# Reciprocal square roots by one third-order step and one Newton step instead of three Newton steps

## The chip, the cores and the metric

The kernel runs on one core of a Trainium2 chip. The metric is the time on the device in microseconds (us); the median of several runs counts. The profile names the engines: PE is TensorE (its weight loads are PEld), DVE is VectorE, ACT is ScalarE, POOL is GpSimd, SP is SyncE, which issues most of the transfers.

## What is computed

The reference is one layer of an encoder over 2048 positions of width 1024. `x` goes through an RMS norm and one input projection. That yields queries, keys and values of two attention mixers (A: a window of 128; B: three groups of heads with dilations 1, 4 and 16), gate paths and merge gates. Every head's query and key has an RMS norm of its own:

```python
def rms_norm(x, gain):
    xf = x.astype(jnp.float32)
    y = xf * lax.rsqrt(jnp.mean(xf * xf, axis=-1, keepdims=True) + EPS)
    return (y * gain.astype(jnp.float32)).astype(x.dtype)

h = rms_norm(x, norm_gain[layer])
proj = h @ w_in[layer]
qa, ka, va, qb, kb, vb, ga, gb, mg = jnp.split(proj, split_idx, axis=-1)
qa = head_rms_norm(qa.reshape(bsz, S, A_Q_HEADS, HEAD_DIM), q_norm_a[layer]) * scale
ka = head_rms_norm(ka.reshape(bsz, S, A_KV_HEADS, HEAD_DIM), k_norm_a[layer])
...
merged = gates[:, :, 0] * br_a + gates[:, :, 1] * br_b
x = x + merged @ w_out[layer]
```

The reciprocal square root of these norms is what the change touches.

## The kernel before

All matmuls take float16 operands, and a float32 operand is split into a high and a low part (`wh`, `wl` for weights, `XH`, `XL` for the normed and transposed `x`), so that one product becomes three.

**The start.** `x` comes in 16 tiles of 128 rows. ScalarE squares a tile and sums its rows (L450), VectorE turns the sums into means and makes a first guess of the root from the bits of the number (L454, `rs_guess` L263), `x_newton` refines it (`rs_newton`), VectorE scales the tile (`x_scale`, L464), TensorE transposes it (L470), ScalarE and VectorE write the high and the low part (L473, L477). The roots are made in five groups: tiles 0 and 1, tiles 2 and 3 (both on VectorE, `pool` False), then four tiles each (on GpSimd, `pool` True).

**The main part** goes through 14 units (two of mixer A, twelve of mixer B), each with 8 pairs of blocks of 128 rows: 112 pairs. For a pair TensorE projects two blocks into two PSUM banks (L655, 48 matmuls). Then follows one round of small work, planned in `Pair.plan`:

- ScalarE copies queries and keys out (L673) and the high part of the values (L688); VectorE writes the low part of the values (`v_lo`, L694), which is the last reader of the PSUM bank;
- ScalarE squares (L701), VectorE sums per head (L706, L707) and makes the guess (L263);
- GpSimd refines the root (`newton`, L272 to L275), 12 instructions on 8 or 10 numbers a partition; the last writes `qr`;
- VectorE multiplies by it (`scale`, L718), GpSimd by the gain (L725), ScalarE and VectorE split the product (L731, L735), GpSimd swaps two halves (L740), and a transposing DMA writes the result into the ring `kq`, out of which ScalarE copies an edge (L758, L764).

Meanwhile the items of the attention run: scores on TensorE (L833), bias and maximum on VectorE (L848), the exponential on ScalarE (L856), a split (L861, L865), a transposing DMA, the products with the values on TensorE (L882), and merges of the heads (GpSimd L1001, L1041; VectorE L1023 to L1048). GpSimd also multiplies the next unit's weights by the gain (`gains`, L182) and those of gate columns (L326). Between the pairs of some units stand whole gate projections (`FILLS`, L310).

**The order.** Everything between `order.enter_context(tc.manual_schedule())` and the end is issued in an order written out by hand: `at(t, f)` puts a step on a heap under a planned time `t` counted in pairs, and `until(t)` issues all steps that are due. Each engine works through its instructions strictly in that order; the planned times decide nothing else. The delays of a pair's steps after its second block are

```python
NORM = (0.028, 0.136, 0.32, 0.626, 0.744, 0.904, 0.962, 1.033, 1.118)
...
steps = (self.square, self.stats, self.newton, self.scale, self.gain, self.hi, self.lo, self.swap, self.turn)
for d, f in zip(NORM, steps):
    at(e[1] + d, f)
```

so that on VectorE the split L735 of one pair stands ahead of L694 and L706 of the next, and L718 ahead of L735.

**The end** (from some 1378 us) makes the rest of the gates, the branch products and the output projection, by TensorE products of half blocks (L1440, L1645), without any of the roots above.

Of the kernel before, what the change touches and what calls it, by code (L numbers as in the profile page):

```python
# [25 lines left out]
OP = mybir.AluOpType  # L26
# [87 lines left out]
def block_kernel(tc, x, w_units, w_gate, w_mrg, w_brn, w_out, w_bra, gain, qkg, sink, bias_a, bias_b, b_merge, out):  # L114
    nc = tc.nc
    V = nc.vector
    A = nc.scalar
    G = nc.gpsimd
# [147 lines left out]
    def rs_newton(a, yv, r, n, pool):  # L266

        t = sm.tile([128, 10], F32, name="rs_t")
        tv = t[:, :n]
        for i in range(3):  # L270
            if pool:
                G.tensor_tensor(tv, yv, yv, OP.mult)  # L272
                G.tensor_tensor(tv, tv, a, OP.mult)  # L273
                G.tensor_scalar(tv, tv, -0.5, 1.5, OP.mult, OP.add)  # L274
                G.tensor_tensor(r if i == 2 else yv, tv, yv, OP.mult)  # L275
                continue
            V.tensor_tensor(tv, yv, yv, OP.mult)
            V.scalar_tensor_tensor(tv, tv, -0.5, a, OP.mult, OP.mult)
            V.scalar_tensor_tensor(r if i == 2 else yv, tv, 1.5, yv, OP.add, OP.mult)


    zd = [dr.tile([2, S, 132], F32, name=f"zd{p}") for p in range(4)]
# [174 lines left out]
    def x_newton(g):  # L457
        ss, y = xss[g]
        xss[g] = sm.tile([128, 4], F32, name="xr")
        rs_newton(ss, y, xss[g][:, :len(g)], len(g), len(g) > 2)  # L460
# [178 lines left out]
    class Pair:  # L639
# [70 lines left out]
        def newton(self):  # L710
            n = 2 * self.nh
            self.rr = sm.tile([128, 10], F32, name="qr")
            rs_newton(*self.ss, self.rr[:, :n], n, True)
# [1064 lines left out]
```

## Time and profile before

| | |
|---|---|
| median of 3 runs | 1948.53 us (1947.81 to 1949.16) |
| profiled execution | 1949.46 us |
| its span, first to last instruction | 1947.7 us |
| mean granted TensorE clock | 0.996 |
| L272, GpSimd | 345 instructions, median 202 ns, 104.9 us busy in all |
| L273, GpSimd | 345, medians 204 and 201 ns |
| L274, GpSimd | 345, median 198 ns |
| L275, GpSimd | 345, medians 200 to 203 ns |
| L277 to L279, VectorE | 18, medians 160 to 161 ns |
| GpSimd's idle time ahead of L272, for the guess L263 | 153.1 us in 86 waits |
| GpSimd's idle time ahead of L725, for L718 | 62.1 us in 69 waits |

The page gives for each engine its busy time and the share of the span; the chain that ended last follows the work back from the last instruction, at each step to what released it. A row of the timeline has the start, the duration, engine, line, operation, and the tile written `<-` those read; in brackets stands how long the engine was idle before it and what released it. A row of waits has the sum, the number and the longest of the waits. A row of windows has the length of the window, then for PE, PEld, DVE, ACT and POOL the busy time and, in brackets, the instructions, then the granted TensorE clock, the share of the DMA engines and GB/s.

### The profile page before, as it was taken

The page shows a single profiled execution, that of the slowest core. Times are in us where ns is not written, and L with a number is a line of the kernel's source. Part 1 is how long each engine was busy: PE and PEld are TensorE (multiplying, and loading weights), DVE is VectorE, ACT ScalarE, POOL GpSimd, SP SyncE. Part 2 cuts the span into 40 slices and gives each one's busy share as a digit, 9 for nine tenths or more (in the row PEclk, how much of TensorE's full clock was granted, in tenths as well). Part 3 has the DMA queues.
Part 4 walks back from the last instruction along what each step waited for, and adds up shares of the span by engine and source line. Part 5 has one row for each costly group of instructions (what it writes and reads, how often), then busy time and mean ns, then how long its engine had stood idle before and what let it go on. Part 6 is the DMA issues. An engine that isn't in the chain of part 4 may idle for free.

```text
span 1947.7 us, 40273 instructions
## 1 busy us (share of the span) xinstructions
PE 1923.5 (99%) x13702; PEld 1211.9 (62%) x13702; DVE 1373.0 (70%) x3604; ACT 1073.4 (55%) x2451; POOL 953.4 (49%) x2440
## 2 busy tenths in 40 slices
PE   7999999999999999999999999999999999999999
PEld 5556676677766688566787567876544444444444
DVE  6668787888767776677876878768776756876422
ACT  7457666776565566665666656666534545422100
POOL 4254456445546756647666676656511310232533
PEclk8999999999999999999999999999999999999999
DMA  6239977797858596677767776765822246778763
GB/s 252 82 75 174 192 154 158 137 188 147 189 96 189 117 189 124 127 147 163 159 130 147 138 173 123 144 120 115 187 82 96 99 157 202 217 236 269 248 243 140
DMA packets 589743, 307.96 MB, mean 158 GB/s; under 512 B 458081, under 2 KB 527329, under 8 KB 588257
## 3 DMA queue, kind: packets, MB, share of 16 engines
q1 hardware_dynamic: 571104, 296.73, 64.7%
q10 hardware_dynamic: 18432, 8.66, 1.9%
q8 instruction: 107, 1.75, 0.4%
q14 instruction: 100, 0.81, 0.1%
HBM read 129.91 MB, written 65.27 MB: 100 GB/s over the span
## 4 chain that ended last, share of the span: by engine, by line
PE 49%; DVE 4%; POOL 3%; issue 2%; ACT 1%; DMA 1%; SPq 0%; DVEq 0%; POOLq 0%
PE pj L655 16%; PE fps L310 13%; PE fps L1645 7%; PE pj L310 6%; PE fps L1440 5%; PE s L833 1%; PE pv L882 1%; POOL rs_t L272 1%; POOL rs_t L273 1%; DVE rw L718 1%; DVE qss L706 1%; POOL rs_t L274 1%; DMA kq<-spl 0%; POOL rs_y L275 0%; DVE pr L848 0%
## 5 line engine op out<-in xcount | busy, mean ns | idle before, releaser
L655 PE MATMUL pj<-wh,XH 128*128 128x384 f16 x1792 | 584.7, 326 | 6.2 <-DVE vt L694 6.2
L655 PE MATMUL pj<-wh,XL 128*128 128x384 f16 x1792 | 586.6, 327 | 0.0
L655 PE MATMUL pj<-wl,XH 128*128 128x384 f16 x1792 | 585.2, 327 | 0.0
L655 PEld LDWEIGHTS <-XH 128*128 128x128 f16 x3584 | 412.9, 117 | 155.1 <-issue 8.1
L848 DVE CUSTOM_DVE_ANT_0 pr<-s,b,ubuf 128x256 f32<-128x256 f32 (+3 forms) x512 | 218.4, 463 | 51.3 <-PE s L833 49.9
L655 PEld LDWEIGHTS <-XL 128*128 128x128 f16 x1792 | 207.8, 116 | 68.8 <-issue 0.2
L272 POOL TENSOR_TENSOR rs_t<-rs_y 128x8 f32<-128x8 f32 (+2 forms) x345 | 104.9, 304 | 211.9 <-DVE rs_y L263 153.1
L865 DVE SCALAR_TENSOR_TENSOR p<-pr,p 128x512 f16<-128x512 f32 (+2 forms) x256 | 185.9, 726 | 25.1 <-ACT p L861 24.2
L718 DVE TENSOR_TENSOR rw<-rw,qr 128x512 f32<-128x512 f32 (+1 forms) x112 | 110.8, 989 | 88.0 <-POOL vt L681 56.9
L725 POOL TENSOR_TENSOR rw<-rw,g 128x128 f32<-128x128 f32 (+1 forms) x224 | 128.9, 596 | 76.5 <-DVE rw L718 62.1
L310 PEld LDWEIGHTS <-wh 128*128 128x128 f16 x960 | 93.8, 98 | 111.4 <-issue 1.5
L861 ACT ACTIVATE p<-pr 128x512 f16<-128x512 f32 (+2 forms) x256 | 159.2, 622 | 6.3
L740 POOL COPY spl<-spl 128x256 f16<-128x256 f16 (+1 forms) x224 | 93.5, 447 | 130.4 <-DVE spl L735 128.9
L310 PE MATMUL fps<-Y,wh 128*128 128x512 f16 x512 | 152.3, 379 | 0.0
L833 PE MATMUL s<-kq 128*128 128x256 f16 (+3 forms) x1168 | 147.8, 254 | 2.0 <-ACT kq L758 2.0
L882 PEld LDWEIGHTS <-pt 128*128 128x128 f16 x3024 | 126.0, 98 | 35.0 <-issue 0.3
L310 PE MATMUL pj<-XH,gl 128*128 128x512 f16 x384 | 146.0, 380 | 0.0
L310 PE MATMUL pj<-XH,gh 128*128 128x512 f16 x384 | 146.0, 380 | 0.0
L310 PE MATMUL pj<-XL,gh 128*128 128x512 f16 x384 | 145.9, 380 | 0.0
L673 ACT ACTIVATE rw<-pj 128x256 f32<-128x256 f32 (+1 forms) x224 | 86.3, 385 | 107.8 <-PE pj L655 94.9
L1645 PE MATMUL fps<-wt,M 128*128 128x512 f16 (+1 forms) x684 | 145.2, 375 | 0.0
L731 ACT ACTIVATE spl<-rw 128x512 f16<-128x512 f32 (+1 forms) x112 | 72.1, 644 | 122.3 <-POOL vt L681 80.5
(245 smaller groups left out, 3679.9 us busy)
## 6 DMA issues: line engine op xcount, KB each, us to landing
wraw<-in_w_units_dram SPq DMA_DIRECT2D x56, 384.0 KB, 4.9
mtd<-mm SPq DMA_DIRECT2D x56, 256.0 KB, 3.8
M<-mtd SPq DMA_DIRECT2D x8, 1792.0 KB, 9.2
mgd<-fg SPq DMA_DIRECT2D x39, 256.0 KB, 2.1
zd<-z ACTq DMA_DIRECT2D x128, 66.0 KB, 2.5
zz<-zd SPq DMA_DIRECT2D x64, 132.0 KB, 2.8
xt<-in_x_dram SPq DMA_DIRECT2D x16, 512.0 KB, 8.6
gtd<-yo SPq DMA_DIRECT2D x32, 256.0 KB, 2.8
```

The source lines that it names most:

```text
L272: G.tensor_tensor(tv, yv, yv, OP.mult)
L310: out.append(lambda w=w, xx=xx, ch=ch, i=i: T.matmul(ps[:], lhsT=w[:, ch, c0:c0 + 128], rhs=xx[:, ch, ts], start=(i == 0), stop=(i == n - 1)))
L655: out.append(lambda lhs=lhs, rhs=rhs, ch=ch, k=k: T.matmul(ps[:, :384], lhsT=lhs[:, ch, :], rhs=rhs[:, ch, :], start=(k == 0), stop=(k == ...
L718: V.tensor_tensor(q, q, self.rr[:, :n].unsqueeze(2).to_broadcast([128, n, HD]), OP.mult)
L725: G.tensor_tensor(q[:, i, :un.nq, :], q[:, i, :un.nq, :], g, OP.mult)
L833: T.matmul(self.sv[j][:, o:o + k1 - k0], lhsT=q[:, h, qo:qo + 128], rhs=kt[:, un.nq + kh + v * un.nk, k0:k1], start=(v == 0), stop=(v == 1))
L848: V.tensor_tensor_reduce(out=self.pv[:, j, self.p0:self.p0 + W], in0=self.sv[j], in1=un.bias[:, self.h0 + j, self.b0:self.b0 + W], scale=I ...
L861: A.activation(self.sp[:, :128 * n], self.pr, AF.Copy, scale=PSC)
L865: V.scalar_tensor_tensor(self.sp[:, 128 * n:], self.pr, PSC, self.sp[:, :128 * n], OP.mult, OP.subtract)
L882: T.matmul(self.po[:, j, :w], lhsT=p[:, n * j + s, :], rhs=un.v[key][:, vh, c0:c0 + w], start=(k == 0 and s == 0), stop=(k == 2 and s == n ...
L1440: mm.append(lambda ch=ch, k=k, w=w, i=i: T.matmul(ps[:], lhsT=weight(bl, ch)[w], rhs=xblock(x, ch)[k], start=(i == 0), stop=(i == 11)))
L1645: mm.append(lambda ch=ch, k=k, w=w, i=i: T.matmul(ps[:, :cols.stop - cols.start], lhsT=m[:, a, ch, k, :], rhs=wt[w][:, b, ch, cols], start ...
```

## The change

`rs_newton` gets the mean `a` and a guess `yv` of its reciprocal square root. Before, it makes three times the step y = y (1.5 - 0.5 a y y). Now, with t = a y y, it makes one step y = y (1.875 - 1.25 t + 0.375 t t) and then one step as before. On GpSimd the twelve instructions become ten, with `r` as a place for what lies between; on VectorE, where an instruction can do two operations on three operands, nine become seven. Nothing else changes, and no other line is moved in the written order.

```diff
         t = sm.tile([128, 10], F32, name="rs_t")
         tv = t[:, :n]
-        for i in range(3):
-            if pool:
-                G.tensor_tensor(tv, yv, yv, OP.mult)
-                G.tensor_tensor(tv, tv, a, OP.mult)
-                G.tensor_scalar(tv, tv, -0.5, 1.5, OP.mult, OP.add)
-                G.tensor_tensor(r if i == 2 else yv, tv, yv, OP.mult)
-                continue
-            V.tensor_tensor(tv, yv, yv, OP.mult)
-            V.scalar_tensor_tensor(tv, tv, -0.5, a, OP.mult, OP.mult)
-            V.scalar_tensor_tensor(r if i == 2 else yv, tv, 1.5, yv, OP.add, OP.mult)
+        if pool:
+            G.tensor_tensor(tv, yv, yv, OP.mult)
+            G.tensor_tensor(tv, tv, a, OP.mult)
+            G.tensor_scalar(r, tv, 0.375, -1.25, OP.mult, OP.add)
+            G.tensor_tensor(r, r, tv, OP.mult)
+            G.tensor_scalar(r, r, 1.875, None, OP.add)
+            G.tensor_tensor(yv, r, yv, OP.mult)
+            G.tensor_tensor(tv, yv, yv, OP.mult)
+            G.tensor_tensor(tv, tv, a, OP.mult)
+            G.tensor_scalar(tv, tv, -0.5, 1.5, OP.mult, OP.add)
+            G.tensor_tensor(r, tv, yv, OP.mult)
+            return
+        V.tensor_tensor(tv, yv, yv, OP.mult)
+        V.scalar_tensor_tensor(tv, tv, 0.375 ** 0.5, a, OP.mult, OP.mult)
+        V.scalar_tensor_tensor(tv, tv, -1.25 * 0.375 ** -0.5, tv, OP.add, OP.mult)
+        V.scalar_tensor_tensor(yv, tv, 1.875, yv, OP.add, OP.mult)
+        V.tensor_tensor(tv, yv, yv, OP.mult)
+        V.scalar_tensor_tensor(tv, tv, -0.5, a, OP.mult, OP.mult)
+        V.scalar_tensor_tensor(r, tv, 1.5, yv, OP.add, OP.mult)
```

## The prediction

> **What bounds the kernel now.** I read the page first: its busy times, then its chain that ended last.
>
> ```profile
> span 1947.7 us, 40273 instructions
> ...
> PE 1923.5 (99%) x13702; PEld 1211.9 (62%) x13702; DVE 1373.0 (70%) x3604; ACT 1073.4 (55%) x2451; POOL 953.4 (49%) x2440
> ...
> PE 49%; DVE 4%; POOL 3%; issue 2%; ACT 1%; DMA 1%; SPq 0%; DVEq 0%; POOLq 0%
> PE pj L655 16%; PE fps L310 13%; PE fps L1645 7%; PE pj L310 6%; PE fps L1440 5%; PE s L833 1%; PE pv L882 1%; POOL rs_t L272 1%; POOL rs_t L273 1%; DVE rw L718 1%; DVE qss L706 1%; POOL rs_t L274 1%; DMA kq<-spl 0%; POOL rs_y L275 0%; DVE pr L848 0%
> ```
>
> TensorE is busy for 99% of the span: at most some 24 us of the whole can be won by anything that leaves its matmuls alone. But the lines of the reciprocal square root on GpSimd (L272 to L275) stand in the chain with about 1% each, so in some stretches TensorE does wait for them. To find the stretches I asked for TensorE's waits in three windows: 60 to 1000 us, 1000 to 1200, 1200 to 1450.
>
> ```profile
> PE pj L655 <- DVE vt L694: 0.7, 2, 0.4
> ```
> ```profile
> PE pj L655 <- DVE vt L694: 3.6, 3, 2.0
> PE s L833 <- ACT kq L758: 1.7, 2, 1.2
> ```
> ```profile
> PE pj L655 <- DVE vt L694: 1.9, 1, 1.9
> PE pt L944 <- DVE ya L1048: 0.7, 1, 0.7
> PE s L833 <- ACT kq L758: 0.3, 1, 0.3
> ```
>
> L694 frees the projection's PSUM bank. VectorE runs in the written order, and there L694 stands behind L718, which multiplies by the result `qr`. L758 copies transposed keys that come out of the same round. So these 8.9 us (0.7 + 3.6 + 1.7 + 1.9 + 0.7 + 0.3) of TensorE's idleness are the prize. What L718 waits for:
>
> ```profile
>   POOL vt L681: 56.9, 37
> ```
>
> The memset L681 is queued right behind the last step of the root; L718 starts at that step's end (below, 1075.80 + 0.20 against 1076.04), so the row is a wait for `qr` under another name.
>
> The chain that ended last, in the windows 1050 to 1130 and 1280 to 1380, leaves TensorE and returns to it as follows; between the two ends stand whole roots on GpSimd.
>
> ```profile
> 1059.72 0.20 PE pv L882 x6
> ...
> 1062.74 0.32 POOL rs_t L272
> ...
> 1114.05 0.20 POOL rs_t L272
> ...
> 1125.33 1.30 PE pj L655 x7
> ```
> ```profile
> 1283.79 0.20 PE pv L882 x6
> ...
> 1286.33 0.32 POOL rs_t L272
> ...
> 1361.16 0.20 POOL rs_t L272
> ...
> 1377.40 0.62 PE s L833 x8
> ```
>
> From 1062.74 to 1114.05 it passes six roots, from 1286.33 to 1361.16 nine (one of them for three steps only). A round (row sums, guess, root, scale, gain, split, and the next row sums behind it on VectorE) takes (1114.05 - 1062.74) / 5 = 10.3 us there and (1361.16 - 1286.33) / 8 = 9.4 in the second stretch; TensorE went through ten pairs before at 8.9 us each (1066.39 - 977.45, rows below), so the rounds are the slower part.
>
> **The change, part by part.**
>
> **GpSimd.** Twelve instructions become ten: seven tensor by tensor and three tensor by scalar where there were nine and three. Their price, from the timeline of one root:
>
> ```profile
> 1072.58 0.31 POOL L272 TENSOR_TENSOR rs_t<-rs_y 128x8 f32<-128x8 f32 x1 [0.40 <-DVE rs_y L263]
> ...
> 1073.26 0.20 POOL L274 TENSOR_SCALAR rs_t<-rs_t 128x8 f32<-128x8 f32 x1
> ...
> 1073.82 0.20 POOL L272 TENSOR_TENSOR rs_t<-rs_y 128x8 f32<-128x8 f32 x1
> ...
> 1075.80 0.20 POOL L275 TENSOR_TENSOR qr<-rs_t,rs_y 128x8 f32<-128x8 f32 x1
> ```
>
> From the fifth to the twelfth start are 1.98 us for seven steps, 0.283 us a step, whichever of the two kinds. Two steps fewer are 0.57 us a root: 3.43 becomes 2.86 us. Where VectorE stretches a step of the root, the stretch belongs to the VectorE instruction beside it and not to the number of steps, so I keep 0.57 everywhere. The one-operation tensor by scalar (add 1.875, no second operation) stands in no row; I take it at the 0.20 of L274, and for its ends 0.1 either way (0.1 x 15 roots = 1.5 us at the most). That `r` is now written from the third step on could add a wait only for the L718 that reads the same buffer, four pairs back; at 8.9 us a pair that is long done: nothing.
>
> **VectorE** (the first two x groups, two tiles each): nine become seven.
>
> ```profile
> 7.52 0.16 DVE L277 TENSOR_TENSOR rs_t<-rs_y 128x2 f32<-128x2 f32 x1
> ...
> 9.09 0.16 DVE L279 SCALAR_TENSOR_TENSOR xr<-rs_t,rs_y 128x2 f32<-128x2 f32 x1
> ```
> ```profile
> 11.99 1.06 ACT L450 ACTIVATE jk<-xt 128x1024 f16<-128x1024 f32 x1 [1.69 <-DMA xt<-in_x_dram]
> ```
>
> Eight steps in 1.57 us are 0.196 each, so 0.39 us a group. What hides it is ScalarE: it splits the first tile only behind the square that stands at 11.99 and waits for a load, and that load does not come sooner. I cost it at nothing; without that cover it would be 0.4 to 0.8 us.
>
> **The third x group, on GpSimd,** is not hidden:
>
> ```profile
> 25.64 1.49 DVE L464 TENSOR_SCALAR xt<-xt,xr 128x1024 f32<-128x1024 f32 x1 [1.72 <-POOL xr L275]
> ```
> ```profile
> 27.27 0.30 PE L470 MATMUL s<-idf,xt 128*128 128x128 f32 x1 [1.93 <-DVE xt L464]
> ```
>
> VectorE waits 1.72 us for the root and TensorE 1.93 us for VectorE; both shrink by 0.57. I count 0.6 us.
>
> **The stretch 1059 to 1125.** Its six roots alone give 6 x 0.57 = 3.4 us. It gives more, because the rounds were already falling behind before TensorE first stood still:
>
> ```profile
> 977.45 0.33 PE L655 MATMUL pj<-wh,XH 128*128 128x384 f16 x1
> ```
> ```profile
> 978.75 0.69 DVE L706 TENSOR_REDUCE qss<-spl 128x8 f32<-128x512 f32 x1 [0.23 <-ACT spl L701]
> ```
> ```profile
> 1066.39 0.33 PE L655 MATMUL pj<-wh,XH 128*128 128x384 f16 x1
> ```
> ```profile
> 1071.35 0.67 DVE L706 TENSOR_REDUCE qss<-spl 128x8 f32<-128x512 f32 x1
> ```
>
> The row sums L706 came 1.3 us after the next pair's first matmul at 977, and 5.0 us after it ten pairs later. Ten roots less by 0.57 are 5.7 us, more than the 3.7 lost; but a round that has caught up can't run ahead of TensorE, so part of that is wasted. I estimate that 2.3 of the 3.7 us are gone by 1071. Five more roots up to the release at 1125.33 add 2.85: the chain arrives 5.2 us sooner. The waits of the window sum to 5.3 (3.6 + 1.7), and a short spell at half clock adds to what TensorE could give back, so the chain, not TensorE, still sets that end: 5.2 us. Ends: 3.4 and 7.0. Late next there: L694 behind L735, as now, by a fraction.
>
> **The stretch 1284 to 1377.** Eight whole roots are 4.6 us, the waits there 1.9 + 0.7 + 0.3 = 2.9. TensorE is the limit: 2.9. If L1048 and the key transposes are late for another reason, 1.9.
>
> **The two early waits** (0.7 us in 60 to 1000): one root each covers 0.4; 0.7. Other end 0.
>
> **All other roots** lie beside a busy TensorE: nothing. Their cover is the 99%; without it they would be 0.57 each.
>
> **The clock.** Half clock shows in two windows of 3.4 us:
>
> ```profile
> 1110.10:1113.60 3.50, 1.51 (x10) 0.78 (x8) 3.43 (x10) 2.61 (x8) 1.89 (x5) 1.00 0.65 137
> 1113.60:1117.00 3.40, 3.40 (x23) 2.28 (x22) 3.03 (x15) 3.14 (x9) 2.29 (x9) 0.50 1.09 101
> ```
> ```profile
> 24.70:28.10 3.40, 1.47 (x12) 1.01 (x11) 2.46 (x3) 1.17 (x3) 1.63 (x5) 1.00 1.03 391
> 28.10:31.50 3.40, 3.40 (x14) 2.00 (x12) 2.24 (x10) 3.25 (x7) 0.00 (x0) 0.51 1.03 399
> ```
>
> In each, a window with TensorE busy for about 1.5 us is followed by one at half clock, which costs 1.7 us of matmuls. The first spell I have inside the 7.0 above. The second may go, since TensorE would be busy 0.57 us longer in the window before it; I leave it out of the sum and put 1.7 into the range. The Trainium skill, "TensorE: Matmul & The Clock Gate", section "What's actually happening", says that the clock falls to half after at least one idle window of about 3.4 us, and that this window runs free of the kernel's start. Its length agrees with the rows; its condition does not (1.5 us of 3.4 were busy). By its condition alone neither spell would be there and 1.7 us less would be at stake; the sum stays as it is.
>
> Sum: 0.6 + 5.2 + 2.9 + 0.7 = 9.4 us. The profiled execution took 1949.46 us, 0.93 above the runs' median of 1948.53. Less 9.4 that is 1940.1, or 1939.1 from the median; I say 1939.5. A measurement tells about 0.2%, 3.9 us, from no change.
>
> **Rivals.**
>
> *TensorE-bound, nothing comes of it.* For it: 99% busy, and TensorE's listed waits are short. Against it: both chains above run through GpSimd. It would leave the start alone, 1948.53 - 0.6 = 1947.9.
>
> *A smaller gain.* The rounds before 1059 win nothing that lasts, the early waits stay, and in the late stretch only L694's wait goes: 3.4 + 1.9 = 5.3, so 1943.2. For it: the key transposes (DMA) stand in the late chain.
>
> *A larger gain.* All waits and both spells go: 0.6 + 1.7 + 7.0 + 2.9 + 0.7 = 12.9, so 1935.6.
>
> *Slower: VectorE's scale is stretched more often.* L718 beside another GpSimd multiplication and alone:
>
> ```profile
> 1066.17 1.47 POOL L182 TENSOR_TENSOR wraw<-wraw,gn 128x768 f32<-128x768 f32 x1
> ```
> ```profile
> 1066.21 1.98 DVE L718 TENSOR_TENSOR rw<-rw,qr 128x512 f32<-128x512 f32 x1 [1.91 <-POOL vt L681]
> 1076.04 0.69 DVE L718 TENSOR_TENSOR rw<-rw,qr 128x512 f32<-128x512 f32 x1 [2.33 <-POOL vt L681]
> ```
>
> A root that ends sooner lets the next GpSimd instruction start sooner. If that puts a weight multiplication beside L718, or beside another VectorE instruction of the round, where there is none now, the round loses 1.98 - 0.69 = 1.29 and wins 0.57. In all fifteen roots of the two chains that is 15 x 0.72 = 10.8, less the 1.3 of start and early waits: 1958.0. It decides from eleven such rounds on (11 x 1.29 = 14.2 against 9.4 + 3.9). Against it: where L718 waits for `qr`, both engines' next work moves by the same 0.57, and their order in time stays. The Trainium skill, "SBUF — State Buffer", section "Who interferes with whom", has the rule behind this: a VectorE instruction with two inputs in SBUF and a GpSimd instruction that reads SBUF exclude each other, the later one waiting for the earlier one's end. The trace agrees: 1.47 + 0.69 = 2.16 in turn, 1.98 measured.
>
> **How the numbers follow.** Chances: the forecast 0.46, the smaller gain 0.20, the larger 0.15, nothing 0.14, slower 0.05. Of the first three all but 0.01 lie over 3.9 us: faster 0.80, within 0.15, slower 0.05. The range runs from the larger gain, 1935.5, past the smaller to 1945.5, and leaves out most of "nothing" and the slower case. The forecast's own ends: 1936 to 1943.
>
> **What would show it.** Right: a root of ten steps in 2.9 us; `xr` ready by 25.1 us and the transpose by 26.8; under 1 us of waits for L694 in all; no more chain through L272 to L275 between 1284 and 1377, and shorter passages before 1125. Wrong: steps longer than 0.283 us, L694 waited for as before, or new L718 durations near 2 us. What would break it: waits that move to L1048 or the key transposes by as much.

## The result, and the profile after

The changed kernel takes 1937.75 us (median of 6 runs, 1937.26 to 1941.01) where the kernel before took 1948.17 beside it (6 runs, 1945.95 to 1949.51): the ratio over all runs is 0.9951, 95% interval 0.9938 to 0.9963 (the two medians alone give 0.9947). That is 10.4 us less; the forecast was 1939.5. The profiled execution is the longest of the six, 1941.01 us with a span of 1939.2.

The page after, span, busy times and the chain that ended last:

```profile
span 1939.2 us, 40047 instructions
...
PE 1921.7 (99%) x13702; PEld 1211.1 (62%) x13702; DVE 1377.2 (71%) x3600; ACT 1075.9 (55%) x2451; POOL 900.6 (46%) x2210
...
PE 88%; DVE 4%; DMA 3%; issue 2%; POOL 1%; ACT 1%; SPq 1%; ACTq 0%; DVEq 0%; POOLq 0%
PE pj L664 41%; PE pj L319 14%; PE fps L319 10%; PE fps L1654 7%; PE s L842 5%; PE fps L1449 5%; PE pv L891 4%; PE pt L953 1%; PE s L479 1%; DMA fg<-ytd 1%; DMA xt<-in_x_dram 0%; DMA kq<-spl 0%; DVE rw L727 0%; DVE qss L715 0%; DMA b<-in_bias_a_dram 0%
```

TensorE has as much work as before. GpSimd has 52.8 us less (953.4 - 900.6), but only the lost time of TensorE counts, and the 8.5 us by which the span is shorter are a sixth of that. The root's lines, three of which held 1% of the chain each, are gone from the list, and GpSimd's share of the chain went from 3% to 1%. The lines behind the root's function moved by 9 (L694 is now L703, L718 L727, L833 L842).

TensorE's waits after, in the windows 60 to 1000, 1000 to 1200 and 1200 to 1450 us:

```profile
PE pt L196 <- DVE yo L960: 0.5, 1, 0.5
...
PE pj L664 <- DVE vt L703: 2.5, 2, 2.1
...
PE s L842 <- ACT kq L767: 0.4, 1, 0.4
PE s L842 <- DMA kq<-spl: 0.2, 1, 0.2
```

The waits for L703 (L694) were 0.7 + 3.6 + 1.9 = 6.2 us and are 2.5, all of it in one stretch. The waits for the key transposes in 1000 to 1200 (1.7) and for L1048 (0.7) are gone.

The chain after, pieces of the windows 1040 to 1130 and 1270 to 1372:

```profile
1058.13 0.32 POOL rs_t L271
...
1087.09 2.65 DMA zz<-zd
...
1106.77 0.20 POOL rs_t L271
...
1110.07 2.20 DMA zz<-zd
...
1115.47 1.20 DVE gl L365
1116.66 0.60 DVE spl L744
...
1117.52 2.08 PE pj L664 x7
...
1346.52 2.60 PE pj L664 x16
...
1353.59 0.68 POOL qr L275
...
1363.40 4.38 DMA kq<-spl
...
1368.16 0.62 PE s L842 x8
```

The release at 1117.52 is the one that stood at 1125.33, the scores at 1368.16 those of 1377.40. The six roots of the first stretch, which began at 1062.74, 1072.58, 1081.10, 1091.01, 1101.48 and 1114.05, now begin 4.61, 5.15, 5.66, 6.18, 6.77 and 7.28 us sooner, and the release comes 7.81 sooner: each round adds the half microsecond of one root. The stretch still ends outside TensorE, but behind the first four steps of the last root the chain now goes through a transfer of the head sums (`zz`), then the low part of a gate's weights (L365), the split L744 and L703. The second stretch stays in TensorE up to about 1349 and passes one whole root instead of eight.

### The profile page after: what moved, and what is told of

Same layout as the page of the kernel before. It is cut to its first block, busy times and chain, and to the rows that moved or that the text cites. A ratio compares the mean times of both kernels' runs of the same rounds, so it can differ in the third digit from the quotient of the medians.

```text
span 1939.2 us, 40047 instructions
## 1 busy us (share of the span) xinstructions
PE 1921.7 (99%) x13702; PEld 1211.1 (62%) x13702; DVE 1377.2 (71%) x3600; ACT 1075.9 (55%) x2451; POOL 900.6 (46%) x2210
## 4 chain that ended last, share of the span: by engine, by line
PE 88%; DVE 4%; DMA 3%; issue 2%; POOL 1%; ACT 1%; SPq 1%; ACTq 0%; DVEq 0%; POOLq 0%
PE pj L664 41%; PE pj L319 14%; PE fps L319 10%; PE fps L1654 7%; PE s L842 5%; PE fps L1449 5%; PE pv L891 4%; PE pt L953 1%; PE s L479 1%; DMA fg<-ytd 1%; DMA xt<-in_x_dram 0%; DMA kq<-spl 0%; DVE rw L727 0%; DVE qss L715 0%; DMA b<-in_bias_a_dram 0%
## 5 line engine op out<-in xcount | busy, mean ns | idle before, releaser
L842 PE MATMUL s<-kq 128*128 128x256 f16 (+3 forms) x1168 | 148.3, 254 | 0.6 <-ACT kq L767 0.4
L271 POOL TENSOR_TENSOR rs_t<-rs_y 128x8 f32<-128x8 f32 (+2 forms) x115 | 40.7, 354 | 212.6 <-DVE rs_y L263 164.5
L891 PE MATMUL pv<-vt,pt 128*128 128x65 f16 (+1 forms) x2784 | 131.6, 193 | 0.0
L182 POOL TENSOR_TENSOR wraw<-wraw,gn 128x768 f32<-128x768 f32 (+1 forms) x80 | 110.1, 1383 | 42.9 <-DVE Y L410 24.7
```

The source lines that it names most:

```text
L182: G.tensor_tensor(v, v, gn[:, c0:c0 + 2].unsqueeze(2).to_broadcast([128, 2, n]), OP.mult)
L842: T.matmul(self.sv[j][:, o:o + k1 - k0], lhsT=q[:, h, qo:qo + 128], rhs=kt[:, un.nq + kh + v * un.nk, k0:k1], start=(v == 0), stop=(v == 1))
L891: T.matmul(self.po[:, j, :w], lhsT=p[:, n * j + s, :], rhs=un.v[key][:, vh, c0:c0 + w], start=(k == 0 and s == 0), stop=(k == 2 and s == n ...
```

## The experiments

The profiled executions are laid beside each other by the start of the same matmul. The table gives by how many us each came sooner than in the kernel before: L655's matmul at 977.45, the release at 1125.33, the scores at 1377.40, and the span of 1947.7.

| kernel | at 977.45 | at 1125.33 | at 1377.40 | span |
|---|---|---|---|---|
| changed, first profile | 2.92 | 7.81 | 9.24 | 8.5 |
| changed, second profile (e12) | 3.35 | 8.27 | 11.33 | 10.7 |
| e1, pairs only | 2.90 | 7.57 | 10.69 | 10.7 |
| e2, 33 late pairs only | 1.02 | 5.92 | 9.02 | 9.1 |
| e3, the other roots only | 2.92 | 2.91 | 2.88 | 3.0 |
| e10, gate part later | 3.40 | 9.59 | 12.79 | 12.9 |

**e1_pairs_only: the x groups keep three Newton steps.**

```diff
-        rs_newton(ss, y, xss[g][:, :len(g)], len(g), len(g) > 2)
+        rs_newton3(ss, y, xss[g][:, :len(g)], len(g), len(g) > 2)
```

> The 112 roots of the pairs are the new ones, the five x groups keep three Newton steps. Theory (latency of the roots that stand in the chain): only the third x group's root was in the chain at the start, so the time is 0.5 to 0.6 us above the changed kernel, about 9.5 us below before, ratio near 0.995. Rival (the start wins by the clock spell that is missing in the changed kernel's profile): 2 to 2.5 us above the changed kernel, 8 us below before.

Measured: 1939.34 us (1938.34 to 1940.33), ratio 0.9944 (0.9932 to 0.9957). That is 10.55 us under the kernel before, as much as the changed kernel wins: the gain lies in the pairs' roots, and the 0.5 to 0.6 us expected for the start can't be seen in the times. In the trace TensorE's wait for the scaled tile is 1.93 us as before. At 977.45 the profile is 0.45 us behind the second of the changed kernel but only 0.02 behind the first, whose loads of `x` came late; the next section shows the start's part without the loads.

**e2_late_pairs and e3_other_roots: the new root in pairs 72 to 87 and 95 to 111 alone, and in all others alone.** These 33 pairs are those of the two stretches.

```diff
+            late = 72 <= self.no < 88 or self.no >= 95
-            rs_newton(*self.ss, self.rr[:, :n], n, True)
+            (rs_newton if late else rs_newton3)(*self.ss, self.rr[:, :n], n, True)
```

> The new root only in the pairs 72 to 87 and 95 to 111 (counted from 0), three Newton steps in all others and in the x groups. Theory: these hold all fifteen roots of the two chains and the rounds that fell behind ahead of them; 3.4 to 5.2 us of the first stretch and 2.7 to 2.9 of the second come back, 6 to 8 us below before (ratio 0.9960 to 0.9968). Rival (the gain is spread over the whole main part, or is made at the start): 33 of 112 pairs give under a third, 1 to 3 us.

> The reverse: three Newton steps in the pairs 72 to 87 and 95 to 111, the new root in the other 79 pairs and in the x groups. Theory: start 0.6 and the early waits 0.7 to 1.7, so 1 to 3 us below before (ratio 0.9985 to 0.9995). Rival (spread gain): two thirds of it, 6 to 7 us. With the run before it the two gains should add up to the whole, 9 to 10 us, if the chains are apart.

Measured: e2 1941.5 us (1939.89 to 1943.66), ratio 0.9956 (0.9944 to 0.9969); e3 1946.47 (1945.47 to 1947.97), 0.9983 (0.9974 to 0.9992). Against 1949.89 beside them that is 8.4 and 3.4 us, each a little more than expected. The chain's pieces where it returns to TensorE, first of e2, then of e3:

```profile
1119.41 1.30 PE pj L682 x7
...
1368.38 0.62 PE s L861 x8
```
```profile
1122.42 1.30 PE pj L682 x7
...
1374.52 0.62 PE s L861 x8
```

e2 comes 1.02 us sooner into the first stretch, and gains 4.90 in it and 3.10 in the second; the changed kernel (second profile) gains 4.92 and 3.06 there. e3 comes in 2.92 sooner and gains nothing in either (2.91, 2.88). So the two stretches, 33 of 112 roots, give 8.0 us, and the other 79 roots give them nothing. The two spans together are 12.1 us shorter where the changed kernel's second profile is 10.7; the spell at half clock at 28 us, 1.7 us in the kernel before, is absent from both and so counts twice.

**e4_two_behind: the changed kernel with two more multiplications behind each root**, which nobody waits for: GpSimd does twelve steps again, the result is there after ten.

```diff
             G.tensor_tensor(r, tv, yv, OP.mult)
+            for _ in range(2):
+                G.tensor_tensor(tv, tv, tv, OP.mult)
             return
```

> The changed kernel with two more multiplications of the scratch tile on GpSimd behind each root, so GpSimd issues twelve instructions again but the result is ready after ten. Theory (latency up to the result counts, not GpSimd's time): VectorE's scale takes longer than the two added steps before GpSimd gets its next input, so most of the gain stays; only where the head merge's products stand right behind the root (four rounds of the two chains) are 0.57 us each lost: 7 to 9.5 us below before. Rival (GpSimd's load counts): all of the gain is gone, within 1 us of before.

Measured: 1944.67 us (1943.5 to 1945.75), ratio 0.997 (0.996 to 0.9981): 5.2 us under the kernel before, between what was expected and what the rival said. The price of the pair was wrong. GpSimd's and VectorE's timelines of e4:

```profile
1091.88 1.64 POOL L282 TENSOR_TENSOR rs_t<-rs_t 128x8 f32<-128x8 f32 x2
...
1101.28 1.31 POOL L282 TENSOR_TENSOR rs_t<-rs_t 128x8 f32<-128x8 f32 x2
```
```profile
1091.84 0.69 DVE L729 TENSOR_TENSOR rw<-rw,qr 128x512 f32<-128x512 f32 x1 [0.21 <-POOL qr L280]
1092.45 1.01 DVE L244 SCALAR_TENSOR_TENSOR wl<-wraw,ubuf,wh 128x768 f16<-128x768 f32 x1
```

The shortest pairs, 35 of the 115, take 0.48 us; these two take 1.64 and 1.31, and the median is 0.99. The first begins together with the scale L729 and ends 0.06 us behind the end of the VectorE instruction after that (1093.52 against 1093.46). The Trainium skill, "SBUF — State Buffer", section "Who interferes with whom", has two such instructions, VectorE's with two inputs in SBUF and GpSimd's reading SBUF, exclude each other; these rows agree with it, as if each small step waited for one VectorE instruction. No run tests that by itself. A step directly behind the result meets the scale that the result has just released.

**e11_memsets_behind: ten memsets instead of the two multiplications**, GpSimd work that reads no SBUF.

```diff
+            for _ in range(10):
+                G.memset(tv, 0.0)
             return
```

> The changed kernel with ten memsets of the scratch tile on GpSimd behind each root, 0.1 us each by the row of the memsets of the value tiles, less where they overlap: 0.5 to 1 us of GpSimd behind the result, that reads no SBUF. Theory (the two multiplications behind the root cost 5 us because they read SBUF while VectorE's scale reads two inputs, and each holds up the other): the memsets cost less, 0 to 2.5 us above the changed kernel. Rival (the time of GpSimd behind the result counts, whatever it does): 4 to 7 us above, as with the multiplications.

Measured: 1955.12 us (1951.75 to 1956.37), ratio 1.0026 (1.0016 to 1.0036), 17 us above the changed kernel beside it: both expectations missed, since the price was wrong again. GpSimd's timeline of e11:

```profile
1069.73 1.56 POOL L282 MEMSET rs_t<- 128x8 f32 x10
...
1071.29 1.48 POOL L182 TENSOR_TENSOR wraw<-wraw,gn 128x768 f32<-128x768 f32 x1
1072.72 0.86 POOL L736 TENSOR_TENSOR rw<-rw,g 128x128 f32<-128x128 f32 x2
```

Ten memsets take 1.56 us, three times the 0.52 by which a root got shorter, and in GpSimd's order the multiplication by the gain (L736) of the same round stands behind them. So time directly behind the result is in the round too. e4 and e11 together do not give a clean split between "the result is there sooner" and "GpSimd is free sooner"; they show that time behind the result is not free, whatever fills it. What share of the change's gain is the one and what the other stays open.

**e5_fourteen and e6_six: the length of the root on a scale.** e5 is the kernel before with two more steps at the end of each root; e6 is the changed kernel without the Newton step on GpSimd (one step less, so a less exact root).

```diff
+                if i == 2:
+                    for _ in range(2):
+                        G.tensor_scalar(r, r, 1.0, 0.0, OP.mult, OP.add)
```
```diff
-            G.tensor_tensor(yv, r, yv, OP.mult)
-            G.tensor_tensor(tv, yv, yv, OP.mult)
-            G.tensor_tensor(tv, tv, a, OP.mult)
-            G.tensor_scalar(tv, tv, -0.5, 1.5, OP.mult, OP.add)
-            G.tensor_tensor(r, tv, yv, OP.mult)
+            G.tensor_tensor(r, r, yv, OP.mult)
```

> The kernel before with two more steps (times 1, plus 0) at the end of each root on GpSimd, fourteen in all. Theory (latency of the rounds): in the two stretches the fifteen roots of the chain cost 0.57 us more each, 8.6 us, and rounds ahead of them that just kept up fall behind too, with 0.6 at the start: 9 to 13 us above before (ratio 1.0045 to 1.007). Rival (TensorE-bound, the change won by the clock or by a lighter GpSimd): 0 to 3 us above.

> The changed kernel without the Newton step of GpSimd's roots: six steps, the output is less exact. Theory: the rounds are 1.1 us shorter than in the changed kernel; what is left to win is the wait of 2.1 us at 1117, 0.6 for the keys at the end of the second stretch, 1.1 at the start, 0.5 at an early wait, and a clock spell of 1.5 us in some runs. So 3 to 5.5 us below the changed kernel (ratio to before 0.9925 to 0.9935), because TensorE is then the limit nearly everywhere. Rival (each step counts as before): fifteen roots by 1.1 us, 15 us or more below the changed kernel.

Measured: e5 1976.37 us (1975.63 to 1978.54), ratio 1.014 (1.0126 to 1.0154); e6 1932.93 (1932.57 to 1933.19), 0.9915 (0.9902 to 0.9929). The chain by engine on the pages of e5 and e6:

```profile
PE 70%; POOL 9%; DVE 9%; issue 6%; DMA 3%; ACT 3%; SPq 0%; POOLq 0%; DVEq 0%; ACTq 0%
```
```profile
PE 96%; DVE 2%; DMA 1%; ACT 0%; issue 0%; SPq 0%; POOL 0%; DVEq 0%; ACTq 0%; POOLq 0%
```

Against the kernel before beside each, 6, 10, 12 and 14 steps give -16.5, -10.95 (e12), 0 and +26.9 us: 1.4 us a step from 6 to 10, 5.5 from 10 to 12, 13.5 from 12 to 14. e5 cost more than twice what was expected because rounds outside the two stretches, which just kept pace, fell behind as well: 8.0 of the 26.1 us by which its span is longer are lost between 35 and 977.45, and its waits for the value split in 60 to 1000 us are 6.5 (0.7 before), in 1200 to 1450 7.1 (1.9 before). e6 lies 5.55 us below the changed kernel, at the upper end of what was expected; with six steps TensorE has no listed wait between 60 and 1200. The start follows the same scale; TensorE's wait for the scaled tile, in the timelines of e5 and e6:

```profile
28.30 0.63 PE L473 MATMUL s<-idf,xt 128*128 128x128 f32 x4 [2.49 <-DVE xt L467]
```
```profile
25.90 0.63 PE L475 MATMUL s<-idf,xt 128*128 128x128 f32 x4 [0.28 <-DVE xt L469]
```

It is 2.49 us with fourteen steps, 1.93 with twelve, 1.41 with ten, 0.28 with six.

**e8_vector_late: the changed kernel with the roots of those 33 pairs on VectorE**, seven steps instead of ten.

```diff
+            late = 72 <= self.no < 88 or self.no >= 95
-            rs_newton(*self.ss, self.rr[:, :n], n, True)
+            rs_newton(*self.ss, self.rr[:, :n], n, not late)
```

> The changed kernel with the roots of the pairs 72 to 87 and 95 to 111 on VectorE (seven instructions of 0.2 us, 1.4 us, and no way to GpSimd and back). Theory: a root gets 1.6 us shorter, but VectorE loses the 0.5 to 1.8 us of other work that it did beside it; rounds in which it waited for the root gain up to 1 us, those of the head merges lose as much. Within 3 us of the changed kernel, either way. Rival (only the root's latency counts): the rounds stop being the limit, 3 to 5 us below the changed kernel.

Measured: 1947.69 us (1946.19 to 1948.69), ratio 0.999 (0.9981 to 0.9999), some 9 us above the changed kernel: missed. VectorE's timeline of e8:

```profile
1086.58 0.16 DVE L282 TENSOR_TENSOR rs_t<-rs_y 128x8 f32<-128x8 f32 x1
...
1087.78 0.17 DVE L288 SCALAR_TENSOR_TENSOR qr<-rs_t,rs_y 128x8 f32<-128x8 f32 x1
...
1095.91 0.69 DVE L878 SCALAR_TENSOR_TENSOR p<-pr,p 128x512 f16<-128x512 f32 x1
1096.51 0.61 DVE L282 TENSOR_TENSOR rs_t<-rs_y 128x8 f32<-128x8 f32 x1
1097.15 0.54 DVE L283 SCALAR_TENSOR_TENSOR rs_t<-rs_t,qss 128x8 f32<-128x8 f32 x1
```

A root alone is short there, 1.37 us instead of 2.91. But it stands in the order of VectorE, which is itself in the chain, behind work such as L878 and ahead of the attention's maxima and of L706; and some steps are stretched to 0.54 and 0.61 us. TensorE's waits of e8 in 1000 to 1200 and 1200 to 1450 show the key copies late again, by 5.0 us where the first profile after has 0.4 for L767 (the waits for L706, 5.4 in all, have grown too, from 2.5):

```profile
PE s L846 <- ACT kq L771: 2.0, 1, 2.0
...
PE s L846 <- ACT kq L771: 3.0, 2, 2.3
```


**e9_gate_low_later and e10_gate_low_later_12: what is late next.** The wait of 2.1 us that stayed ends behind L365, L744 and L703 in VectorE's order. Both move the planned time of the gate's low part (L365) by 0.218 of a pair, so that L744 and L703 go ahead of it; e10 leaves the last unit as it was.

```diff
-G_PREP = (5.907, 6.882, 7.102, 7.671, 7.712, 7.812, 7.942)
+G_PREP = (5.907, 6.882, 7.102, 7.671, 7.712, 7.812, 8.16)
```
```diff
-              + [(t + d, f, c) for d, f in zip(G_PREP[2:], (g_square, g_sum, g_pow, g_hi, g_lo))])
+              + [(t + d + (.218 if f is g_lo and u < 13 else 0), f, c)
+                 for d, f in zip(G_PREP[2:], (g_square, g_sum, g_pow, g_hi, g_lo))])
```

> The changed kernel with one planned time moved: the low part of the gate columns (VectorE, 1.28 us) is written out behind the next pair's row sums and guess (8.16) instead of ahead of the split and of the release of the PSUM bank (7.942). Theory: the chain's end at 1117 and the key copy at the end of the second stretch stand behind that instruction in VectorE's order; they come 1.2 us sooner each: 1.5 to 3 us below the changed kernel, ratio to before 0.9935 to 0.9945. Rival (the wait at 1117 has another cause, the transfer of the heads' parts for instance): no change against the changed kernel, ratio 0.9945 to 0.995.

> The changed kernel with the low part of the gate columns written later in all units but the last, whose time stays. Theory: the wait of 2.1 us at 1117 is 0.9 as in the run that moved all of them, and the key copy that came 1.1 us later there is back at 0.4: 1 to 2.5 us below the changed kernel. Rival (what is won at 1117 is lost behind it): within 0.5 us of the changed kernel.

Measured: e9 1938.19 us (1938.14 to 1939.29), ratio 0.9945 (0.9932 to 0.9959); e10 1936.74 (1936.58 to 1937.31), 0.9936 (0.9923 to 0.995). TensorE's waits in 1000 to 1200 and 1200 to 1450, of e9 and of e10:

```profile
PE pj L664 <- DVE vt L703: 1.3, 2, 0.9
...
PE s L842 <- ACT kq L767: 1.5, 1, 1.5
```
```profile
PE pj L664 <- DVE vt L703: 1.2, 2, 0.9
...
PE s L842 <- ACT kq L767: 0.3, 1, 0.3
```

In both, the wait of 2.1 is 0.9. In e9 the copy of the last unit's keys is then waited for 1.1 us longer, which takes the gain back: its ratio is no better than the changed kernel's, and its expectation was missed. e10 avoids it. e10 is 1.4 us under the changed kernel beside it, with ranges that do not overlap: the fastest version here with the full root of ten steps, 12.4 us under the kernel before. So the gate's low part was the next thing late.

**e12_changed_again: the changed kernel beside e10 and e11.**

> The changed kernel itself, as the yardstick for the two others on the same chip: 0.9945 to 0.9955 of before.

Measured: 1938.17 us (1937.62 to 1939.47), ratio 0.9944 (0.9932 to 0.9957). Its value is its trace, which shows much the same waits as the first without its spell at half clock (next section).

## Why the prediction was right, point by point

The sum was 9.4 us; 10.4 and 10.95 were measured. The second profile of the changed kernel against the first of the kernel before, by the forecast's terms:

| term | forecast | shown |
|---|---|---|
| up to 977.45: third x group and early waits | 0.6 + 0.7 | 3.35: 0.3 up to the transpose, 1.7 a spell at half clock that is absent, 1.4 from there |
| stretch 1059 to 1125 | 5.2 | 4.92 |
| stretch 1284 to 1377 | 2.9 | 3.06 |
| behind 1377 | 0 | -0.6 |
| sum | 9.4 | 10.7 |

Without the absent spell the profile shows 9.0. That this is so near to 9.4 is partly luck: TensorE came 0.4 us further ahead of 977.45 than forecast and lost 0.6 behind 1377, where no term stood, and the two nearly cancel.

**The root.** Mechanism right, size a little off. One root after, GpSimd's timeline:

```profile
1067.43 0.32 POOL L271 TENSOR_TENSOR rs_t<-rs_y 128x8 f32<-128x8 f32 x1 [0.39 <-DVE rs_y L263]
...
1068.69 0.24 POOL L275 TENSOR_SCALAR qr<-qr 128x8 f32<-128x8 f32 x1
1069.01 0.20 POOL L276 TENSOR_TENSOR rs_y<-qr,rs_y 128x8 f32<-128x8 f32 x1
...
1070.14 0.20 POOL L280 TENSOR_TENSOR qr<-rs_t,rs_y 128x8 f32<-128x8 f32 x1
```

From 1067.43 to 1070.34 are 2.91 us, forecast 2.86. The one-operation tensor by scalar, which no row showed, takes 0.24 us, and 0.32 to the next start (1069.01), where 0.20 and 0.283 were taken; a root saves 0.52, not 0.57.

**The start.** `xr` was to be ready by 25.1 us and the transpose to come by 26.8. In the first profile they came at 26.07 and 27.73, since the loads of x were a microsecond later (ScalarE's square that waits for one began at 12.96, not 11.99). What the term is about, the two waits, is as forecast:

```profile
26.10 1.49 DVE L473 TENSOR_SCALAR xt<-xt,xr 128x1024 f32<-128x1024 f32 x1 [1.20 <-POOL xr L280]
```
```profile
27.73 0.63 PE L479 MATMUL s<-idf,xt 128*128 128x128 f32 x4 [1.41 <-DVE xt L473]
```

1.72 became 1.20 and 1.93 became 1.41, 0.52 each. From the matmul that stands at 24.75 in the kernel before to the transpose at 27.27, both profiles of the changed kernel gain 0.52 us and e1 and e2, with the old root there, nothing.

**The stretch 1059 to 1125** was to end 5.2 us sooner and does by 4.89 and 4.92 in the two profiles of the changed kernel, 4.90 in e2 and 4.67 in e1. e2 shows that its own roots do this, not those long before it. The estimate inside, that 2.3 us of the lost pace are back by the root at 1072.58, came out at 2.23 (5.15 - 2.92). The step on "late next" was too mild: not L694 behind L735 by a fraction, but behind L356 (now L365) as well, which stood in the chain before too, 1.20 us long, and the wait there stayed at 2.1 us. So "under 1 us of waits for L694 in all" was wrong: 2.5.

**The stretch 1284 to 1377**: forecast 2.9, shown 3.06; TensorE sets it, as said. "No more chain through L272 to L275" holds but for one root at its end.

**The early waits.** Waits for L694 went from 0.7 to 0 in one profile and 0.2 in the other, as costed. The forecast left out the transposes of the results (L196), whose wait of 0.9 us became 0.5 to 0.7. These listed waits shrank by 0.7 in the second profile; the other half of the 1.4 stands in no listed wait.

**The clock** is the part that one profile could not decide. The forecast took the spell at 28.1 to follow from a window in which TensorE was busy for 1.47 us, left it out of the sum and kept it in the range. In each trace the spells begin and end whole multiples of 3.413 us apart (before, 318 of them from 28.14 to 1113.58), so the clock goes by windows of that length, and they lie differently against the program in each execution. Such windows of the changed kernel's first profile, then of e2, whose start is that of the kernel before:

```profile
1114.47:1117.88 3.41, 1.33 (x11) 0.92 (x10) 3.40 (x9) 3.18 (x11) 0.55 (x2) 1.00 0.84 168
1117.88:1121.30 3.42, 3.42 (x14) 1.83 (x13) 3.21 (x15) 0.29 (x2) 2.35 (x10) 0.50 0.92 220
```
```profile
21.95:25.36 3.41, 2.22 (x19) 1.58 (x17) 1.88 (x3) 3.31 (x7) 2.58 (x11) 1.00 1.06 382
25.36:28.78 3.42, 1.60 (x13) 1.31 (x14) 3.23 (x4) 1.19 (x4) 1.13 (x2) 1.00 1.02 390
28.78:32.19 3.41, 3.41 (x23) 2.06 (x22) 3.04 (x12) 3.41 (x7) 0.00 (x0) 1.00 1.01 393
```

In e2 TensorE's idle time at the start is shared out between two windows, and the clock stays full where the kernel before fell to 0.51; e8 and e11, with the new root at the start, have a spell at 24.1 and 23.6. So the 1.7 us that are absent at the start of the changed kernel's profiles can't be put down to the change. The other spell, at 1113.6 before, stands behind the release at 1117.9 in the first profile after and takes back 1.7 of the 7.81 us; the second has the same wait of 2.1 us, but its window has 1.42 us busy and is followed by full clock. Laid out so over all thirteen traces, from the first window at full clock on, the five windows under 1.4 us busy were all followed by half clock, of the fourteen from 1.4 to 1.69 five, and of all the busier ones one (2.00, in e10). What decides between 1.4 and 1.69 stays open.

On the average of many runs the change does go with a higher clock, which fits the forecast's reason: the mean granted clock is 0.9967 over the 45 runs of the kernel before beside the experiments and 0.9982 over the 11 of the changed kernel, of which six show 0.999 and none of those 45. Among runs of one kernel, 0.001 more of clock goes, loosely, with 0.5 us less time; by that, an estimate, the clock is 0.8 us of the gain.

The Trainium skill, "TensorE: Matmul & The Clock Gate", section "What's actually happening", says that the window runs free of the kernel's start; spells on a grid that lies differently in each execution agree with that, while no window here was wholly idle (the least had 0.79 us busy, in e11).

**The rivals.** "Nothing comes of it" and the slower case are out by the measurement. The scale is stretched less, not more; its group by line and form, in the kernel before and in the second profile of the changed one:

```profile
L718 DVE TENSOR_TENSOR rw<-rw,qr 128x512 f32<-128x512 f32 x96 | 93.7, 976 | 81.4 <-POOL vt L681 53.5 <-POOL qr L275 18.5 <-POOL vw L681 8.4
```
```profile
L727 DVE TENSOR_TENSOR rw<-rw,qr 128x512 f32<-128x512 f32 x96 | 88.7, 924 | 24.1 <-POOL vt L690 15.3 <-POOL qr L280 6.9 <-POOL vw L690 1.0
```

Its mean goes from 976 to 924 ns, and VectorE's idle time ahead of it from 81.4 to 24.1 us; that 57 us of it are worth 10 to TensorE says again how much of it was hidden. Of the smaller gain, one step was right: the early rounds give the first stretch nothing (e3). The larger gain needed all waits and both spells away, and 2.1 us of one wait stayed. What broke a little of it is what the forecast named, the key transposes: of the 0.8 and 0.6 us lost behind 1377, 0.4 and 0.7 are lost at one scores matmul that waits for a key transfer, in the first and in the second profile:

```profile
1378.81 0.61 PE L842 MATMUL s<-kq 128*128 128x256 f16 x4 [0.23 <-DMA kq<-spl]
```
```profile
1377.03 0.61 PE L842 MATMUL s<-kq 128*128 128x256 f16 x4 [0.55 <-DMA kq<-spl]
```

e1 and e10 have no such wait and lose nothing there.

## What to carry to other kernels

A shorter step on an engine that is half idle pays only in the stretches where its round runs slower than the bound engine; find them by the waits in windows, and price them by the start of the same matmul rather than by busy time (52.8 us less work gave 10). The worth of a microsecond of latency is not a constant: 1.4 us a step here when most rounds keep pace, 13.5 when more and more of them fall behind. What stands directly behind a result in the same engine's order can belong to the round as well, and the next late piece (here the gate's low part) may be had by one planned time.

## What was not expected of the hardware

- A one-operation tensor by scalar on GpSimd, 128x8 in place, takes 0.24 us and 0.32 to the next start; the two-operation form 0.20 and 0.283.
- Memsets of that size show 0.10 us each but follow each other at 0.16 (ten in 1.56).
- Two GpSimd multiplications that start with VectorE's scale took 1.31 and 1.64 us in the rows shown; the shortest pairs took 0.48.
- Spells at half clock begin on a grid of 3.413 us that lies differently against the program in each execution. All five windows with TensorE busy for less than 1.4 us were followed by one; of the fourteen with 1.4 to 1.69 us five were.
